# Attention layer of a two-layer streaming step: which queue loads what was turned through DRAM, when the values are loaded, and when the second group's outputs are turned

## The chip, the cores and the metric

The kernel runs on one core of one Trainium2 chip. The metric is the device time of one execution in microseconds (us); the time before is the median of three runs. Five engines work side by side, each through its own instructions in order: TensorE (PE in the profile; PEld is its weight load), VectorE (DVE), ScalarE (ACT), GpSimd (POOL) and SyncE (SP). SP computes nothing here: it issues the transfers (DMAs). ACT can issue transfers too, from the same stream of instructions in which its computing stands. A transfer that has to wait for data waits in the stream of the engine that issues it.

## The reference

One inference step of a trunk with two layers, for a prompt of 512 tokens and a sample of 32 (T = 544 columns). Layer 0 mixes tokens by a recurrence (RWKV-7); layer 1, which the change touches, by differential attention. Cut to layer 1:

```python
h = rmsnorm(x, norm_w)
q, k, v, qm, gate = jnp.split(h @ w_in, [MIX_W, 2 * MIX_W, 3 * MIX_W, 3 * MIX_W + MEM_W], axis=-1)
...
attn = probs(q1, k1) - lam * probs(q2, k2)
return jnp.einsum('bhqk,bkhd->bqhd', attn.astype(v_all.dtype), v_all)
...
o = rmsnorm(o, subln) * (1.0 - lam_init)
y_mem = mem_attention(qm, mk, mv)
out = jnp.concatenate([o.reshape(B, T, MIX_W).astype(x.dtype), y_mem], axis=-1) * jax.nn.silu(gate)
return x + out @ w_out, k, v
```

There are 12 heads of 128, in three groups of four; scores are masked to chunks of 64. Four memory heads attend to 256 memory rows.

## The kernel before

**Products.** A projection is three float32r products (high by high, high by low, low by high part) over 8 blocks of 128 rows, for two halves of 272 columns: 48 products for each block of 128 output columns. Each head of layer 1 has blocks for its values, keys and queries, most have a gate block, and heads 1, 3, 5 and 7 have two more for a memory head. So a head takes 144, 192, 240 or 288 products; even heads 0 to 8 take 192.

**The written order.** `diff_layer` (L1809) puts all other work between these products by hand. `at(pos, fn)` (L1817) has `fn` called ahead of product `pos`; `f` is the first product of a head. One loop calls what is due and then issues the next product. With `self.ordered` set, `tie` (L142) keeps each engine's instructions in the order in which they are called: `self.te`, `self.ve`, `self.ae` and `self.se` are the queues of PE, DVE, ACT and SP. All instructions called through these have line L125 in the profile, so that one reads by the names of tiles instead.

**One head.** Scores of four tiles of 128 queries are computed at `f + x`, their exponentials on ACT at `f + x + 6`, and at `f + y` (`TILES1`, L39) DVE joins the two maps and turns the result, the weights, in 32 by 32 blocks into `pk`. The rest of the turn goes through DRAM. With `y` = 280 for the last tile:

- `weights_out` (L1955), 24 products after `y`: four stores `ptr<-pk`;
- `weights_back` (L1964), `BACK1` = 88 after `y`: the values (`values_back`, L1960: `vt<-scr`), then the turned weights (`aT<-ptr`), both issued by SP;
- `weighted` (L1969), `SUMS1` = 160 after `y`: 20 products `ps_o<-vt,aT`, which DVE copies to `ot`.

`vt`, `aT` and the staging tile `to` have one buffer each. Heads 10 and 11 have `BACK2` and `SUMS2`; head 10 stores at 8 after `y`, and head 11 turns its weights on PE and loads its values alone.

Since a head of 192 products ends before `y` + 24, the later steps of a head lie among those of the next: for the even heads the weights are stored at product 112 of the next head, just behind that head's `keys_out` at 108 (`kh<-kh`, two copies, and four stores `scr<-sg`).

**Other turns through DRAM.** DVE turns a tile in blocks into `to`, SP stores it (`spread`, L1784), and SP loads it back: the cached keys (`cached_back`, L2015), the memory heads' weights (`mem_steps`, L1131; four loads `mpT<-mspread` for each of four memory heads, 56 products after the last stores and 62 ahead of their use) and the first group's outputs (`turned_back`, L2088: `oTt<-spread`, 60 products after the stores, 42 ahead of their use in `finished`).

**Outputs.** When a group's four heads are done, `norms` computes their scales at product `b`; `scaled` (L2078) multiplies each head's output `ot` by them, and `finished` (L2092) multiplies it into the gates `og`. The first group is turned through DRAM, the second and third by PE (`ps_oT<-ident,ot`, four transposes per head in one PSUM bank of a pair shared with the memory heads' products, `ps_mo`, and `ps_o`). For the second group `b` is product 76 of head 9; head j is scaled at `b` + 18 + 14j and turned at `b` + 30 + 24j. A memory head's `ps_mo` is written at product 120 of head 9.

Of the kernel before, what the change touches and what calls it, by code (L numbers as in the profile page):

```python
# [17 lines left out]
P = 128  # L18
D = 1024
KT = D // P  # L20
TP = 512
TS = 32
# [12 lines left out]
DH = 12  # L35
# [6 lines left out]
SAMPLE1 = ((310, "s"), (338, "m"), (362, "t"), (386, "w"), (406, "n"), (464, "r"))  # L42
SAMPLE2 = ((186, "s"), (214, "m"), (228, "t"), (264, "w"), (311, "n"), (336, "r"))
TILES2 = ((152, 180), (210, 236), (240, 268), (272, 304))
BACK1, SUMS1, NORM1 = 88, 160, 52
BACK2, SUMS2, NORM2 = 56, 104, 34
SUMS3 = 22
NORM1B = 76
OTURN = 1
# [4 lines left out]
OUT1 = 24  # L54
# [73 lines left out]
class Trunk:  # L128
# [1002 lines left out]
    def mem_steps(self, st, i, h, p):  # L1131
# [64 lines left out]
        else:  # L1196
            pT = p.tile([P, 2, T], F32, tag="mpT", name="mpT")
# [9 lines left out]
        if i and MTURN:  # L1207
            yield
            pT = p.tile([P, 2, T], F32, tag="mpT", name="mpT")
            for j in range(2):  # L1210
                x = scr.rearrange("(t j p) q -> j p t q", j=2, p=P)[j]
                self.se.dma_start(pT[:, j, :TP].rearrange("p (t q) -> p t q", t=4), x[:, :4])
                self.se.dma_start(pT[:, j, TP:], x[:, 4, P - TS :])
        yield
        sg = st["gate"]()
        g = self.dest(12 + h, sg)
# [592 lines left out]
    def diff_layer(self, dq, p, mp, mctx, pool_early, order, made):  # L1809
# [7 lines left out]
        def at(pos, fn):  # L1817
            ev.append((pos, len(ev), fn))
# [13 lines left out]
        def make_v(st):  # L1832
            def make(w):
                st["v"] = dq.tile([P, T], F32, tag="v", name="v", bufs=KB)
                yield from self.steps(w, copied(st["v"]))
            return make

        def make_k(st):
            def make(w):
                st["k"] = dq.tile([P, T], F32, tag="k", name="k", bufs=KB)  # L1840
                yield from self.steps(w, copied(st["k"]))
            return make
# [16 lines left out]
        def make_gate(g):  # L1859
            def make(w):  # L1860
                yield from self.steps(w, self.gate_evac(self.o1[g])[2])
            return make
# [97 lines left out]
        def values_back(st):  # L1960
            st["vt"] = vt = p.tile([P, 4, P], F32, tag="oTt" if st["h"] == DH - 1 else "vt", name="vt", bufs=1)
            self.se.dma_start(vt[:], st["G"]["scr"][1][:TP, st["j"], :].rearrange("(i p) d -> p i d", p=P))

        def weights_back(st):  # L1964
            st["aT"] = aT = p.tile([P, 10, P], F32, tag="aT", name="aT", bufs=1)
            values_back(st)
            self.se.dma_start(aT[:], st["ptr"].rearrange("(i b) t c -> (b t) i c", b=4))

        def weighted(st):  # L1969
            G, j = st["G"], st["j"]  # L1970
# [17 lines left out]
        def opened(G, hg):  # L1988
            G["scr"] = [self.dp.tile([T, 4, P], F32, tag=f"scr{i}", name=f"scr{i}", bufs=3) for i in range(2)]
            G["on"] = []  # L1990
# [23 lines left out]

        def cached_back(G):  # L2015
            ckT = p.tile([P, 4, P], F32, tag="ckT", name="ckT")
            self.se.dma_start(ckT[:], G["ckT"].rearrange("(j d) q -> d j q", d=P))
            G["ckT"] = ckT

        def sample_scores(G):  # L2020
# [66 lines left out]

        def turned_back(G, j):  # L2088
            G["oT", j] = x = p.tile([P, 4, P], F32, tag="oTt", name="oTt", bufs=1)
            self.se.dma_start(x[:], G["ot", j].rearrange("(t d) q -> d t q", d=P))  # L2090

        def finished(G, hg, j):  # L2092
            if hg < OTURN:
                x = G.pop(("oT", j))[:].rearrange("p t q -> p (t q)")
            else:
                ps = self.psm.tile([P, 512], F32, tag="m", name="ps_oT")
                for t in range(4):
                    self.te.transpose(ps[:, t * P : t * P + P], G["on"][j][:, t, :], self.ident[:])
                x = ps[:]
            g = self.o1[4 * hg + j]  # L2100
            self.ve.scalar_tensor_tensor(g[:, :TP], x, self.subs, g[:, :TP], ALU.mult, ALU.mult)
            self.ve.tensor_tensor(g[:, TP:], G["oT"][:, 32 * j : 32 * j + 32], g[:, TP:], ALU.mult)
# [10 lines left out]
        for h, st in enumerate(sts):  # L2113
            f, hg, G = len(makes) * 6 * KT, h // 4, groups[h // 4]
            start.append(f)
            makes += [make_v(st), make_k(st), make_q(st)] + [make_gate(g) for g in GATES1.get(h, ())]
            if h % 4 == 0:
                at(f, lambda G=G, hg=hg: opened(G, hg))
                at(f + 97, lambda G=G: sample_open(G))
                at(f + 152, lambda G=G, hg=hg: cached(G, hg))  # L2120
            if h % 4 == 1:
                for off, fn in ((4, cached_keys), (14, cached_stored), (78, cached_back)) if CTURN else ((124, cached_turned),):
                    at(f + off, lambda G=G, fn=fn: fn(G))
            for off, fn in ((52, values_turn), (62, lambda st: st["vout"]()), (99, keys), (108, keys_out)):
                at(f + off, lambda st=st, fn=fn: fn(st))
            last = h == DH - 1
            for t, (x, y) in enumerate(TILES2 if last else TILES1):
                at(f + x, lambda st=st, t=t: scores(st, t))
                at(f + x + 6, lambda st=st, t=t: powers(st, t))
                at(f + y, lambda st=st, t=t, fn=joined if last else turned: fn(st, t))  # L2130
                if last:
                    at(f + y + 12, lambda st=st, t=t: turned_here(st, t))
            back, sums = (BACK2, SUMS2) if h >= DH - 2 else (BACK1, SUMS1)
            for off, fn in ((124, values_back),) if last else ((y + (8 if h == DH - 2 else OUT1), weights_out), (y + back, weights_back)):
                at(f + off, lambda st=st, fn=fn: fn(st))
            at(f + y + (SUMS3 if last else sums), lambda st=st: weighted(st))
            at(f + y + (SUMS3 + 11 if last else sums + 14), lambda st=st: squared(st))
            if h in MEM1:
                m = MEM1.index(h)
                makes += [make_query(mems[m]), make_mem_gate(mems[m], m)]  # L2140
                for off in MEMAT1:
                    at(f + off, lambda m=m: next(mits[m], None))
            if h % 4 == 3:
                for off, fn in (SAMPLE2 if last else SAMPLE1):
                    fn = {"s": sample_scores, "m": sample_mixed, "t": sample_turned, "w": sample_weighted, "n": sample_norm, "r": sample_rows}[fn]
                    at(f + off, lambda G=G, fn=fn: fn(G))
                b = f + y + NORM2 if last else begin(h + 2) + (NORM1 if h < 4 else NORM1B)
                at(b, lambda G=G: norms(G))
                for j in range(4):
                    if hg >= OTURN and not last:  # L2150
                        at(b + 18 + 14 * j, lambda G=G, j=j: scaled(G, j))
                        at(b + 30 + 24 * j, lambda G=G, hg=hg, j=j: finished(G, hg, j))
                    elif last:
                        at(b + 18 + 8 * j, lambda G=G, j=j: scaled(G, j))
                        at(b + 30 + 14 * j, lambda G=G, hg=hg, j=j: finished(G, hg, j))
                    else:
                        x = b + 18 + STEP * j
                        at(x, lambda G=G, j=j: (scaled(G, j), turned_out(G, j)))
                        at(x + 10, lambda G=G, j=j: turned_stored(G, j))
                        at(x + GAP1, lambda G=G, j=j: turned_back(G, j))  # L2160
                        at(x + GAP2, lambda G=G, hg=hg, j=j: finished(G, hg, j))
            if h == 10:
                we = []
                at(f + 34, lambda: (mctx.close(), we.append(pool_early())))
            if h >= 10:
                def early(g):
                    made[g] = self.gated(g, *self.fetch(we[0], g))

                def late(g, n):
                    if n == 3:  # L2170
                        hi, lo = (dq.tile([P, T], F32R, tag=x, name=x + "hl", bufs=KB)[:] for x in "kv")
                    else:
                        t = self.kz[0] if n == 2 else dq.tile([P, 2, T], F32R, tag=("qp", "kh")[n], name="hl", bufs=QB)
                        hi, lo = t[:, 0, :], t[:, 1, :]
                    made[g] = self.gated(g, hi, lo, self.o1[g][:])
                for i in range(2):
                    at(f + 40 + 60 * i, lambda g=order[2 * h - 20 + i]: early(g))
            if last:
                for i in range(4):
                    at(f + LATE[i], lambda g=order[4 + i], i=i: late(g, i))  # L2180
# [102 lines left out]
```

## Time and profile before

| | |
|---|---|
| median of 3 runs | 1376.84 us (1376.33 to 1378.81) |
| the profiled execution's own time | 1376.32 us |
| its span, from the first instruction to the last | 1374.6 us |
| layer 1's attention, by PE's products | about 827 to 1268 us of the span |

The profile is one execution. A row of the timeline has start, duration, engine, line, operation, output<-inputs, shape, count, and in brackets the idle time of the engine before it and what ended it. A row of the chain of waits has start, duration and what the time went to. A row of the windows has the stretch, its length, then for each engine the busy time and the number of instructions, then PE's granted clock, the busy share of the 16 DMA engines and GB/s; it can be made for one tile's instructions alone. A row of waits has who waited for whom, the sum, the count and the longest, in us. Since matmuls are pipelined, products that follow each other closely overlap in the rows: one takes some 290 ns from start to end, but the next starts 125 ns after it.

In the issues of the page, one `aT<-ptr` moves 640 KB, one `vt<-scr` 256 KB, one `ptr<-pk` 160 KB, and the four `mpT<-mspread` of a memory head 256, 16, 256 and 16 KB.

### The profile page before, as it was taken

Reading aid. Unit: us, or ns where it says so; the run is one execution under the profiler, and the core shown is the slowest. Engines: PE = TensorE matmul, PEld = TensorE weight load, DVE = VectorE, ACT = ScalarE, POOL = GpSimd, SP = SyncE. Lnnn points to the kernel's source line nnn. Section 1 sums busy time; section 2 is a strip of 40 time slices with the busy share of each in tenths; the row PEclk is TensorE's granted clock in tenths of the full one; section 3 lists DMA queues with packets and bytes.
Section 4 is the critical chain, followed back from the end, with each engine's and each line's share of the span. In section 5 each row is a group of like instructions: output and inputs, shape, how many; then the busy total and the mean of one; then the engine's idle time right before and its main releaser. Section 6 shows DMA issues by size and latency. Waiting matters only on the chain. (4 is left out here: it accounts for less than half of the span.)

```text
span 1374.6 us, 31283 instructions
## 1 busy us (share of the span) xinstructions
PE 1323.3 (96%) x11584; PEld 1267.4 (92%) x11584; DVE 896.9 (65%) x2207; ACT 773.1 (56%) x2090; POOL 567.3 (41%) x986
## 2 busy tenths in 40 slices
PE   6999999999999999999999999999999999999997
PEld 6998899999999999888899999999999899899997
DVE  7776667877787778756674473555667456767443
ACT  7665677677777776655643354544444354454321
POOL 2317675558556855560130034444343343442000
PEclk9999999999999999999999999999999999999998
DMA  7542223322332232323273457676888688785321
GB/s 237 176 128 68 65 64 83 85 74 64 84 86 73 63 85 76 77 81 110 87 219 122 132 154 185 164 173 163 205 181 182 169 202 184 161 187 171 93 70 65
DMA packets 428850, 173.57 MB, mean 126 GB/s; under 512 B 203721, under 2 KB 413138, under 8 KB 428698
## 3 DMA queue, kind: packets, MB, share of 16 engines
q1 hardware_dynamic: 428554, 171.06, 48.1%
q8 instruction: 91, 1.49, 0.4%
q10 hardware_dynamic: 144, 0.52, 0.1%
q14 instruction: 61, 0.50, 0.1%
HBM read 131.89 MB, written 42.96 MB: 127 GB/s over the span
## 5 line engine op out<-in xcount | busy, mean ns | idle before, releaser
L125 PE MATMUL ps_g<-hl,whi 128*128 128x272 f32 x1872 | 544.4, 294 | 0.6 <-POOL hl L497 0.5
L125 PE MATMUL ps_g<-hh,wlo 128*128 128x272 f32 x1808 | 537.0, 297 | 1.4 <-DVE wlo L125 1.4
L125 PE MATMUL ps_g<-hh,whi 128*128 128x272 f32 x1808 | 536.5, 297 | 0.9 <-ACT hh L125 0.9
L125 PEld LDWEIGHTS ps_g<-hl,whi 128*128 128x128 f32 x1872 | 352.8, 190 | 3.2 <-POOL hl L497 0.7
L125 PEld LDWEIGHTS ps_g<-hh,whi 128*128 128x128 f32 x1808 | 343.3, 190 | 5.3 <-ACT hh L125 1.3
L125 PEld LDWEIGHTS ps_g<-hh,wlo 128*128 128x128 f32 x1808 | 342.8, 190 | 5.7 <-DVE wlo L125 2.2
L125 ACT CAST whi<-raw 128x512 fp32r<-128x512 f32 x322 | 190.9, 619 | 92.4 <-PE ps_g L125 51.3
L786 POOL TENSOR_TENSOR tm<-u,m 102x84 f32<-102x84 f32 (+23 forms) x372 | 154.6, 416 | 167.3 <-DMA m<-sc 139.2
L335 POOL TENSOR_TENSOR wlo<-raw,whi 128x512 fp32r<-128x512 f32 x110 | 142.9, 1316 | 191.4 <-ACT whi L125 168.0
L125 DVE TENSOR_TENSOR wlo<-raw,whi 128x512 fp32r<-128x512 f32 x212 | 153.8, 741 | 65.4 <-ACT whi L125 63.9
L788 POOL TENSOR_TENSOR u<-u,tm 102x84 f32<-102x84 f32 (+23 forms) x372 | 165.5, 445 | 29.1
L125 PE MATMUL ps_g<-lo,whi 128*128 128x272 f32 x448 | 129.3, 289 | 0.7 <-DVE lo L125 0.7
L125 PE MATMUL ps_g<-hi,whi 128*128 128x272 f32 x448 | 129.2, 288 | 0.0
L125 PE MATMUL ps_g<-hi,wlo 128*128 128x272 f32 x448 | 129.1, 288 | 0.0
L125 PEld LDWEIGHTS ps_g<-lo,whi 128*128 128x128 f32 x448 | 84.2, 188 | 1.1 <-DVE lo L125 1.1
L125 PEld LDWEIGHTS ps_g<-hi,whi 128*128 128x128 f32 x448 | 84.3, 188 | 0.0
L125 PEld LDWEIGHTS ps_g<-hi,wlo 128*128 128x128 f32 x448 | 84.3, 188 | 0.0
L125 DVE SCALAR_TENSOR_TENSOR SB<-ps_c,dl,sd 64x64 f32<-64x64 f32 x168 | 47.5, 282 | 45.1 <-PE ps_c L125 40.1
L125 ACT COPY sv<-ps_c 64x64 f32<-64x64 f32 x192 | 39.5, 206 | 37.6 <-PE ps_c L125 35.8
L1882 POOL TENSOR_TENSOR kz<-k,kh 64x544 fp32r<-64x544 f32 x24 | 33.0, 1373 | 51.4 <-ACT kh L125 50.5
L1652 POOL TENSOR_TENSOR hl<-hn,hh 128x544 fp32r<-128x544 f32 x8 | 12.5, 1568 | 92.9 <-ACT hh L125 92.9
L125 DVE SCALAR_TENSOR_TENSOR qp<-ps_g,qp 64x272 fp32r<-64x272 f32 x48 | 21.1, 439 | 41.4 <-ACT qp L125 41.2
(397 smaller groups left out, 2566.0 us busy)
## 6 DMA issues: line engine op xcount, KB each, us to landing
raw<-in_rw_in_dram SPq DMA_DIRECT2D x114, 256.0 KB
raw<-in_df_in_dram SPq DMA_DIRECT2D x112, 256.0 KB
raw<-in_w_out_dram SPq DMA_DIRECT2D x64, 256.0 KB
ptr<-pk SPq DMA_DIRECT2D x44, 160.0 KB
aT<-ptr SPq DMA_DIRECT2D x11, 640.0 KB
scr<-sg SPq DMA_DIRECT2D x96, 68.0 KB
out_dram<-scr SPq DMA_DIRECT2D x6, 1024.0 KB
m<-sc SPq DMA_DIRECT2D x36, 128.0 KB
```

What stands on the lines that cost most here:

```text
L125: return lambda *a, **k: self.trunk.tie(self, issue(*a, **k))
L335: todo.append((lambda k=k, q=q: low.tensor_tensor(lo[:, k], raw[q][:], hi[:, k].bitcast(F32), ALU.subtract), LATER))
L786: nc.gpsimd.tensor_tensor(tm[:, :n, :wd], u3[:, :n, kx : kx + 1].to_broadcast(sh), m3[:, kx : kx + 1, kx + 1 :].to_broadcast(sh), ALU.mult)
L788: nc.gpsimd.tensor_tensor(u3[:, :n, kx + 1 :], u3[:, :n, kx + 1 :], tm[:, :n, :wd], ALU.add)
L1652: nc.gpsimd.tensor_tensor(self.hl[:, k, :], h[:], self.hh[:, k, :].bitcast(F32), ALU.subtract)
L1882: nc.gpsimd.tensor_tensor(self.kz[h % 2][rows[m], m, :], k[rows[m], :], hi.bitcast(F32), ALU.subtract)
```

## The change

Four edits, all in layer 1:

- the loads of `aT`, `mpT`, `ckT` and `oTt` are issued by ACT (`self.ae`) in place of SP (`self.se`), at the same places of the order; `aT`'s load is 4 products earlier (`BACK1` 88 to 84; `BACK2` 56 to 54);
- the values of heads 0 to 10 are loaded 18 products after `y`, in place of `BACK1` or `BACK2`: ahead of the weights' stores, except in head 10, which stores at 8; still by SP;
- head 10's (and only its) `SUMS2` is 112 in place of 104;
- the second group's outputs are turned at `b` + 54 + 24j in place of `b` + 30 + 24j.

```diff
-BACK1, SUMS1, NORM1 = 88, 160, 52
-BACK2, SUMS2, NORM2 = 56, 104, 34
+BACK1, SUMS1, NORM1 = 84, 160, 52
+BACK2, SUMS2, NORM2 = 54, 112, 34
...
-                self.se.dma_start(pT[:, j, :TP].rearrange("p (t q) -> p t q", t=4), x[:, :4])
-                self.se.dma_start(pT[:, j, TP:], x[:, 4, P - TS :])
+                self.ae.dma_start(pT[:, j, :TP].rearrange("p (t q) -> p t q", t=4), x[:, :4])
+                self.ae.dma_start(pT[:, j, TP:], x[:, 4, P - TS :])
...
         def weights_back(st):
             st["aT"] = aT = p.tile([P, 10, P], F32, tag="aT", name="aT", bufs=1)
-            values_back(st)
-            self.se.dma_start(aT[:], st["ptr"].rearrange("(i b) t c -> (b t) i c", b=4))
+            self.ae.dma_start(aT[:], st["ptr"].rearrange("(i b) t c -> (b t) i c", b=4))
...
-            self.se.dma_start(ckT[:], G["ckT"].rearrange("(j d) q -> d j q", d=P))
+            self.ae.dma_start(ckT[:], G["ckT"].rearrange("(j d) q -> d j q", d=P))
...
-            self.se.dma_start(x[:], G["ot", j].rearrange("(t d) q -> d t q", d=P))
+            self.ae.dma_start(x[:], G["ot", j].rearrange("(t d) q -> d t q", d=P))
...
-            for off, fn in ((124, values_back),) if last else ((y + (8 if h == DH - 2 else OUT1), weights_out), (y + back, weights_back)):
+            for off, fn in ((124, values_back),) if last else ((y + min(18, back - 2), values_back), (y + (8 if h == DH - 2 else OUT1), weights_out), (y + back, weights_back)):
...
-                        at(b + 30 + 24 * j, lambda G=G, hg=hg, j=j: finished(G, hg, j))
+                        at(b + 54 + 24 * j, lambda G=G, hg=hg, j=j: finished(G, hg, j))
```

## The prediction

> **What bounds the kernel now.** First the page, then the waits of TensorE (PE) in the attention layer, 826 to 1270 us.
>
> ```profile
> span 1374.6 us, 31283 instructions
> PE 1323.3 (96%) x11584; PEld 1267.4 (92%) x11584; DVE 896.9 (65%) x2207; ACT 773.1 (56%) x2090; POOL 567.3 (41%) x986
> PE ps_o L125 <- DMA aT<-ptr: 4.7, 3, 3.0
> PE ps_oT L125 <- DVE ot L125: 2.3, 2, 1.9
> PE ps_s L125 <- DMA kh<-kh: 0.8, 1, 0.8
> PE ps_oT L125 <- DVE og L125: 0.6, 1, 0.6
> PE ps_s L125 <- ACT pt L125: 0.4, 1, 0.4
> ```
>
> PE is busy for 96%, and its products are issued in one written order. So a saving must come out of the 51 us in which PE is idle, and only 8.8 us of those (the sum of the five wait rows) lie in the layer that the change touches. The timeline of PE places them; the windows view shows what follows the longest.
>
> ```profile
> 920.04 0.30 PE L125 MATMUL ps_s<-kh,qp 128*128 128x128 f32 x1 [0.85 <-DMA kh<-kh]
> 1034.67 0.44 PE L125 MATMUL ps_s<-kh,qp 128*128 128x384 f32 x1 [0.41 <-ACT pt L125]
> 1039.71 2.47 PE L125 MATMUL ps_o<-vt,aT 128*128 128x128 f32 x20 [0.54 <-DMA aT<-ptr]
> 1072.35 3.32 PE L125 MATMUL ps_o<-vt,aT 128*128 128x128 f32 x20 [2.97 <-DMA aT<-ptr]
> 1118.94 2.39 PE L125 MATMUL ps_o<-vt,aT 128*128 128x128 f32 x20
> 1152.49 2.47 PE L125 MATMUL ps_o<-vt,aT 128*128 128x128 f32 x20 [1.22 <-DMA aT<-ptr]
> 1170.88 0.66 PE L125 MATMUL ps_oT<-ident,ot 128*128 128x128 f32 x4 [1.87 <-DVE ot L125]
> 1177.33 0.66 PE L125 MATMUL ps_oT<-ident,ot 128*128 128x128 f32 x4 [0.62 <-DVE og L125]
> ...
> 1020.00:1040.00 20.00, 19.05 (x149) 18.64 (x148) 11.49 (x32) 9.38 (x29) 9.53 (x8) 1.00 0.99 220
> 1060.00:1080.00 20.00, 17.03 (x126) 16.84 (x126) 8.37 (x20) 8.13 (x21) 9.56 (x7) 0.91 0.78 175
> ...
> 1075.67 0.91 PE ps_g L125 x4
> 1042.18 0.76 PE ps_g L125 x6
> ```
>
> In the window that holds the 2.97 us gap the granted clock is 0.91; in the window with the 0.54 us gap it is 1.00. The twenty products behind the long gap take 3.32 us where the undisturbed twenty take 2.39, and four weight products take 0.91 where six took 0.76 (four: 0.51). So this wait costs 2.97 + 0.93 + 0.40, about 4.3 us, not 3.0.
>
> **Why the weights come late.** The timeline of SyncE (SP), heads 4, 5 and 7, and the products that PE ran ahead of head 5's wait:
>
> ```profile
> 1023.42 3.57 SPq L125 DMA_DIRECT2D ptr<-pk  x4
> 1028.08 1.26 SPq L125 DMA_DIRECT2D oTt<-spread  x1
> 1033.58 0.50 SPq L125 DMA_DIRECT2D aT<-ptr  x1
> 1051.37 3.21 SPq L125 DMA_DIRECT2D ptr<-pk  x4
> 1060.79 2.63 SPq L125 DMA_DIRECT2D scr<-sg  x4
> 1063.52 1.87 SPq L125 DMA_DIRECT2D raw<-in_df_in_dram  x1
> 1065.49 0.45 SPq L125 DMA_DIRECT2D vt<-scr  x1
> 1066.00 0.50 SPq L125 DMA_DIRECT2D aT<-ptr  x1
> 1131.95 4.05 SPq L125 DMA_DIRECT2D ptr<-pk  x4
> 1145.54 0.58 SPq L125 DMA_DIRECT2D aT<-ptr  x1
> ...
> 1060.17:1069.40 9.23, 9.21 (x74) 8.99 (x72) 1.31 (x3) 2.03 (x6) 1.00 0.75 172
> ...
> 1066.00 6.22 DMA aT<-ptr
> 1150.69 3.10 DMA mspread<-to
> ```
>
> The load is written 72 products ahead of its use (88 against 160). PE passed that place at 1060.2: the window holds 74 products, two of them at its edges. SP issued it at 1066.00, since it stood behind a store that waited, four stores and a weight load that waited. It landed 6.22 us later, at 1072.2; PE had stood since 1069.4. SP was 5.8 us late, and that, not the transfer alone, is the wait.
>
> **The change, part by part.** (1) *aT to ScalarE's (ACT's) queue*, 11 issues. It now starts when ACT gets to the place and the weights' stores have landed. Store landing isn't a row; the nearest is the 3.10 us of a store out of the same kind of transpose, the far end the 6.22 of aT. Head 5: stores issued by 1054.6, landed about 1057.7. ACT's position:
>
> ```profile
> 1060.20 0.39 ACT L125 COPY k<-ps_g 128x272 f32<-128x272 f32 x1
> 1027.42 0.40 ACT L125 ACTIVATE og<-ps_g 128x272 f32<-128x272 f32 x1
> 1032.59 0.75 DVE L125 SCALAR_TENSOR_TENSOR og<-oTt,dv,og 128x512 f32<-128x512 f32 x1 [3.18 <-DMA oTt<-spread]
> ```
>
> ACT reaches it at 1060.6, the data lands at 1066.8 with the old 6.22, and PE comes at 1069.4: 2.6 us to spare. Head 7: stores issued by 1136.0, landed 1139.1; PE passes the place about 9 us + scores ahead of 1151.3, so the load goes near 1140.5 rather than 1145.54; 6 us later is 4.5 us early. Head 4: stores landed about 1030.1, load then rather than at 1033.58, landing 1036.3 against 1039.2. All three waits go: 0.54 + 2.97 + 1.22 = 4.7 us, and 1.3 us at the low clock with them. Together **6.0** (ends: 2.8, if only the longest shrinks, by half, and the low clock goes with it, and 6.0 itself).
>
> The clock drop is the place to weigh the Trainium skill: its page "TensorE: Matmul & The Clock Gate", section "What's actually happening", has the half rate follow one idle window of about 3.4 us. The 2.97 us gap here is shorter, so by the page the 1.3 us need not go with the wait, and the sum below would be 6.2 in place of 7.5; the trace has the drop behind this gap and none behind those of 1.87 us and less, and I go by the trace.
>
> (2) *Values ahead of the weights' stores* (SP, 11 issues of 0.45 to 0.50 us, some 70 products earlier). Their single buffer is free: the last user's products are written 50 products before, two before in head 10, and SP comes to them no sooner than PE, if it runs as late as at head 5. They put 0.5 us of issue and 256 KB ahead of the stores, so weights land up to 1.5 us later; counted in (5). In odd heads they also stand just ahead of the keys' copies. Head 10's products, 8 later with their load, had no wait: nothing.
>
> (3) *Other loads to ACT*: the first group's outputs (4), cached keys (3), memory weights (16). With aT, SP loses 34 issues of about 0.5 us, 17 us; POOL issues no load in this layer and is passed by none. The outputs' load is the one that now hurts: VectorE stood 3.18 us for it, came late to the scores' maxima, and so PE waited 0.41. It is written 42 products (5.3 us) ahead of its use, which VectorE came to at 1029.4; so ACT issues it near 1024.1 rather than SP at 1028.08, and with the old 4.5 us to its use it is there at 1028.6: **0.4** saved (0 to 0.4). Where SP runs ahead of PE, the memory weights now go later, when ACT gets there; the 62 products (7.8 us) to their use cover the 6.22 us that a load of two and a half times their size takes: nothing, at worst 1 us for each of four heads. The keys' copy behind the wait of 0.85 had the values and weights of the head before just ahead of it on SP; the weights now share the engines instead of standing in front, and I take half: **0.4** (0 to 0.85; in odd heads up to -1).
>
> (4) *Second group's outputs turned 24 products on* (3.0 us, 16 transposes, 8 VectorE instructions, moved past a pair of score tiles; VectorE is busy for 65% of the span).
>
> ```profile
> 1157.44 0.71 DVE L125 STREAM_TRANSPOSE to<-ck 128x512 f32<-128x512 f32 x1 [3.08 <-DMA mspread<-to]
> 1170.09 0.73 DVE L125 TENSOR_TENSOR ot<-ot,oss 128x512 f32<-128x512 f32 x1
> ```
>
> VectorE lost 3.08 us to a store and scaled the first output at 1170.09; PE had come at 1169.0. 3.0 us later the tile is ready with 1.2 us to spare, so 1.87 goes. The 0.62 is a wait for a PSUM bank that the memory head's output still holds, 10 products before; with the new places the first output follows that output by the same 10 products, so half of it may stay. **2.2** (0 to 2.5).
>
> (5) *What ACT pays.* A wait now stands in ACT's stream: behind it are PSUM copies, exponentials and weight casts, for which PE, VectorE and POOL wait. Head 4: ACT is free at 1027.8, the stores land at 1030.1 to 1030.6; held 2.5 us. The far end, 6.22 for the stores, holds it 5.4. The even heads have their stores at the same place, right behind the keys' copies, and are taken alike; head 5 isn't held (1057.7 against 1060.6). PE needs an exponential 32 products (4 us) after its scores, and has three banks of 24 products: 2.5 us mostly fits. I take **-1.5** in all (0 to -6: four heads by 1.5). The issues themselves:
>
> ```profile
> 1260.46 2.01 ACTq L1708 DMA_DIRECT2D fw<-in_final_norm_w_dram  x1
> 1260.66 0.38 ACT L125 ACTIVATE og<-ps_g 128x272 f32<-128x272 f32 x1
> L125 SPq DMA_DIRECT2D aT<-ptr x11: 359/497/579, 878.3 to 1233.5; - x11
> ```
>
> The one issue on ACT took 2.01 us, the same transfers on SP 0.5. ACT went on computing beside its issue, and is idle 44% of the time; I take 0.5 us each, hidden.
>
> **Sum.** 6.0 + 0.4 + 0.4 + 2.2 - 1.5 = 7.5 us off the profiled execution's 1376.32 (1.7 us more than its span): 1368.8. The median shown is 0.5 above that execution: **1369.3**. Ends of this case: 1366.5 to 1372.
>
> **Rivals.**
> *ACT is held longer than PE's banks cover.* The stores land by the 6.22 us row; each of four even heads costs PE 1 to 1.5 us, some 5 us instead of 1.5: 1373. For: the stores are many short runs, and the values now go ahead of them. Against: the 4 us between scores.
> *The loads land no earlier.* In 1020 to 1040 the DMA share is 0.99, so a load issued earlier only queues in the engines. Then (1) shrinks to the issue time of what no longer precedes it, about 1.5 us, (3) gives nothing and (4) 2.2, less 1.5 for ACT: 1374.6. Against: the share around the longest wait is 0.75 to 0.78. The Trainium skill stands with this rival: "DMA: Bandwidth & Descriptors", section "Issuing engines are not separate DMA queues", says that issuing from several engines saves only the sequencer's issue time, usually small. Here that time was 5.8 us for head 5.
> *Slower: ACT's issues cost 2.01 us each.* Four in a row for a memory head hold ACT 8 us, against 6 us of banks: 2 us lost, four times; aT's adds 1.5 us to each of four held heads, beyond the 4 us between scores: 14 us lost against 9.0 gained, and 1381.8. It decides from about 1.2 us an issue. Against: ACT computed beside its 2.01 us.
>
> **Chances.** Forecast 0.62; held longer 0.17; no earlier 0.12; slower 0.09. I count as no change what lies within 0.2% (2.75 us) of 1376.84, about what a measurement of this kernel can tell. The forecast is faster; of the second case 0.13 is faster, 0.04 the same; of the third 0.03 and 0.08, with 0.01 slower. Faster 0.78, same 0.12, slower 0.10. The range of 8 in 10 leaves out the slower case and the upper part of the third: 1365.5 to 1374.5, the low end 1 us below the case's, for the spread of single runs.
>
> **What would show it.** aT on ACT's queue, issued near 1030, 1060 and 1140; no ps_o row with a wait, clock 1.00 throughout; the ps_oT wait of 1.87 gone. Wrong, if PE waits for ACT's exponentials or bank copies behind a load, if aT takes much longer than 6.2 us to land, or if ACT's issue rows are near 2 us.

## The result, and the profile after

The change made the kernel slower: 1391.49 us (median of 4 runs, 1390.65 to 1392.18) against 1377.25 for the kernel before in the same session, a ratio of 1.0104 (1.0090 to 1.0118). The forecast was 1369.3. The profiled execution's span went from 1374.6 to 1389.7 us, 15.1 more. From the first to the last of layer 1's 2688 written products PE took 448.6 us instead of 433.3; what follows them took the same (114.3 and 114.6). That first number, the *layer time*, is read from PE's rows in every run below.

The row of the page on the engines:

```profile
PE 1326.9 (95%) x11584; PEld 1270.1 (91%) x11584; DVE 894.5 (64%) x2207; ACT 771.8 (56%) x2090; POOL 564.7 (41%) x986
```

PE is busy 3.6 us longer for the same products, which is the low clock, and idle for 62.8 us instead of 51.3. Its waits in the attention layer (826 to 1290 us: who waited for whom, sum, count, longest):

```profile
PE ps_o L125 <- DMA aT<-ptr: 7.5, 3, 5.2
PE ps_s L125 <- DMA kh<-kh: 5.9, 5, 2.4
PE ps_o L125 <- issue: 1.7, 1, 1.7
PE ps_g L125 <- DVE srs L125: 1.5, 1, 1.5
PE ps_s L125 <- ACT pt L125: 0.6, 1, 0.6
PE ps_oT L125 <- DVE og L125: 0.5, 1, 0.5
PE ps_oT L125 <- DVE ot L125: 0.2, 1, 0.2
```

The three old waits for `aT` are gone (heads 4, 5 and 7: 0.54, 2.97 and 1.22 us before), and that of 1.87 for `ot`. But the largest row is again `aT`, now in heads 0, 2 and 6 (0.3, 5.2 and 2.0 us), where nothing waited before, and the keys' copies, waited for once and 0.8 us before, are waited for five times. The seven rows make 17.9 us where the five of before made 8.8.

The chain of waits shows the two longest transfers of the turned weights, in heads 2 and 6, and one of keys, in head 8:

```profile
955.56 13.36 DMA aT<-ptr
1120.26 11.42 DMA aT<-ptr
1153.88 5.96 DMA kh<-kh
```

Head 2's load, which in the kernel before took 5.9 us on SP's queue (issued at 953.6, landed at 959.5), took 13.36 us on ACT's. What moved in that stretch, 955.2 to 969 us, stands in the view of the DMA queues (packets, MB, share of the 16 engines; then the issues). q1 carries what SP issues, q10 what ACT issues:

```profile
q1 hardware_dynamic: 3963, 3.62, 78.8%
q10 hardware_dynamic: 1296, 0.66, 16.1%
out_dram<-scr SPq DMA_DIRECT2D x2, 1024.0 KB
raw<-in_df_in_dram SPq DMA_DIRECT2D x3, 256.0 KB
aT<-ptr ACTq DMA_DIRECT2D x1, 640.0 KB
```

So the load met the copies of keys and values to the outputs (`out_dram<-scr`). On a queue of its own it ran *beside* them, and while SP's queue moved 3.62 MB, it got 16% of the engines for its 0.66. In the kernel before, the copies came on SP's queue 10.4 us behind the load, when it had landed. SP's three rows there:

```profile
953.56 0.37 SPq L125 DMA_DIRECT2D aT<-ptr  x1
953.98 9.96 SPq L125 DMA_DIRECT2D raw<-in_df_in_dram  x4
963.99 3.14 SPq L125 DMA_DIRECT2D out_dram<-scr  x4
```

and the copies' row in the changed kernel:

```profile
955.29 3.40 SPq L125 DMA_DIRECT2D out_dram<-scr  x4
```

Between load and copies stood four loads of the projections' weights (`raw`), three of which waited for POOL. The load's leaving is not all that changed here. Counted by the `raw` loads issued ahead of them, the copies of heads 2 and 6 also moved up by three places in SP's own stream. The kernel calls them behind the layer (`kv_out`, when `self.ordered` is off), so that no `tie` holds them at a place. No run has the load on ACT with the copies at their old place.

The second new thing is in SP's waits and ACT's in the layer (826 to 1290 us):

```profile
SPq L125 <- DMA aT<-ptr: 30.7, 7, 7.1
SPq L125 <- DMA oTt<-spread: 3.5, 2, 2.3
SPq L125 <- DMA mpT<-mspread: 3.0, 3, 1.6
SPq L125 <- DMA ckT<-spread: 2.5, 1, 2.5
ACT cmk L125 <- DMA ptr<-pk: 11.6, 3, 5.8
```

SP issues none of these four loads and uses none of their data, yet it stands 39.7 us until they have landed. The events of the trace show why. Each transfer of the two queues counts its end on one of eight semaphores, which the program hands round over both queues: in the kernel before, the 430 transfers issued from 826 to 1260 us use the eight in turn without a break, and in the changed kernel ACT's loads use the same eight. When SP comes to a semaphore whose last transfer was ACT's, its instruction waits until that transfer has landed: each of SP's waits above is for the very semaphore on which its next transfer counts. In the kernel before, where one queue issued everything, SP waited less than 2 us for transfers in this layer.

At last the clock. Windows of PE around head 2's gap and head 6's (columns as before: busy time and count of PE, granted clock, DMA share, GB/s):

```profile
963.00:967.00 4.00, 0.87 (x7) 1.00 1.09 374
967.00:969.00 2.00, 0.00 (x0) 0.51 0.41 123
971.00:974.00 3.00, 3.00 (x16) 0.52 0.08 23
...
1085.00:1087.00 2.00, 1.42 (x9) 0.88 0.86 128
1087.00:1089.00 2.00, 2.00 (x10) 0.50 0.76 195
```

The clock was half from 967.0 to 973.9 us, around the end of the gap of 5.2, and for 3.4 us each behind gaps of 1.33 (head 6's keys) and 2.36 (head 8's).

### The profile page after: what moved, and what is told of

The parts are those of the page before. It is cut to its first block, busy times and chain, and to the rows that moved or that the text cites. A ratio compares the mean times of both kernels' runs of the same rounds, so it can differ in the third digit from the quotient of the medians.

```text
span 1389.7 us, 31324 instructions
## 1 busy us (share of the span) xinstructions
PE 1326.9 (95%) x11584; PEld 1270.1 (91%) x11584; DVE 894.5 (64%) x2207; ACT 771.8 (56%) x2090; POOL 564.7 (41%) x986
## 5 line engine op out<-in xcount | busy, mean ns | idle before, releaser
L788 POOL TENSOR_TENSOR u<-u,tm 102x84 f32<-102x84 f32 (+23 forms) x372 | 160.8, 432 | 29.1
```

The source lines that it names most:

```text
L788: nc.gpsimd.tensor_tensor(u3[:, :n, kx + 1 :], u3[:, :n, kx + 1 :], tm[:, :n, :wd], ALU.add)
```

## The experiments

The theories: **Q**, the load on a second queue shares the engines with what SP's queue has under way, and lands late; **S**, SP waits on the shared semaphores until ACT's loads have landed, and then issues keys and stores late; **H**, ACT, which waits for the stores ahead of its load, comes late with exponentials and copies; **V**, the values in front delay stores and keys.

Each ratio is to the kernel before on the same chip, with its 95% interval. "SP for ACT" is the time that SP waited in the layer for loads issued by ACT. A layer time is that of the one profiled execution, and so less sure than a median: the one of at_act took 1387.19 us and that of sp_copies_last 1367.19, each some 3 us under its median.

| run | median us | ratio | layer time us | SP for ACT us |
|---|---|---|---|---|
| the change | 1391.49 | 1.0104 (1.0090 to 1.0118) | 448.6 | 39.7 |
| sp_all | 1372.50 | 0.9961 (0.9944 to 0.9978) | 429.6 | 0 |
| sp_all_again | 1371.94 | 0.9957 (0.9945 to 0.9970) | 429.8 | 0 |
| at_act | 1390.22 | 1.0099 (1.0069 to 1.0128) | 445.0 | 24.3 |
| others_act | 1378.80 | 1.0010 (0.9995 to 1.0025) | 436.4 | 7.3 |
| turn54 | 1374.69 | 0.9984 (0.9969 to 0.9999) | 430.8 | 0 |
| vals_early | 1374.38 | 0.9986 (0.9977 to 0.9996) | 430.1 | 0 |
| tiny_act | 1377.56 | 1.0005 (0.9994 to 1.0016) | 433.4 | 15.4 |
| tiny_dep | 1370.59 | 0.9958 (0.9943 to 0.9972) | 430.0 | 2.6 |
| after_at_pool | 1412.10 | 1.0256 (1.0241 to 1.0271) | 471.8 | 8.3 |
| copies_last | 1380.64 | 1.0019 (1.0008 to 1.0031) | 436.5 | 24.8 |
| sp_copies_last | 1370.46 | 0.9948 (0.9933 to 0.9963) | 427.0 | 0 |
| best_gap58 | 1370.58 | 0.9953 (0.9939 to 0.9966) | 429.2 | 0 |

### The queue, or the rest of the change: sp_all, at_act, others_act

sp_all is the changed kernel with all four loads back on SP:

```diff
-            self.ae.dma_start(aT[:], st["ptr"].rearrange("(i b) t c -> (b t) i c", b=4))
+            self.se.dma_start(aT[:], st["ptr"].rearrange("(i b) t c -> (b t) i c", b=4))
```

and the same for `mpT`, `ckT` and `oTt`. at_act is the kernel before with this line alone the other way (the values stay right ahead of it, on SP); others_act is the kernel before with the other three loads on ACT.

> The changed kernel with all 34 loads put back on SP's queue; the values ahead of the weights' stores, the 84/54 products and the second group's later turn stay. Theory (the loads on ACT's queue cost the time: SP stands 30.7 us for weights and 9.0 us for the other loads that ACT issued, and the weights land in 7.7 to 13.4 us beside SP's copies): SP's waits for loads are gone, no head's weights take over 7 us, PE's waits for kh are back at about 1 us, the ps_oT wait of 1.87 is gone, and the time is 1372 to 1377, at or below before. Rival (the values ahead of the stores delay the stores and the keys' copies): the PE waits for kh of 5.9 us stay for the most part, and the time is 1383 to 1388.

> The kernel before with one edit: the load of the turned weights (11 issues) is issued by ACT. Theory S (SP waits until a load that ACT issued has landed, where its own next DMA counts on the same semaphore): SP's waits for aT are again some 25 to 35 us, PE waits for kh and for aT, and the time is 1381 to 1387. Theory Q (no more than the loss of the place ahead of SP's copies): aT lands in 8 to 13 us in three or four heads, PE waits for aT 5 to 8 us and for kh as before (1 us), 1379 to 1383. Theory H (ACT held until the stores have landed): PE waits for ACT and VectorE, 2 to 3 us; alone it gives 1375 to 1378, as the waits of 4.7 us for aT go.

> The kernel before with one edit: the first group's turned outputs, the cached keys and the memory weights (23 issues) are issued by ACT, the weights by SP as before. Theory S: SP waits some 9 us for these loads, in short pieces of 1 to 2.5 us, keys come late in one or two heads: 1377 to 1380. Rival (these loads are harmless, and only aT costs): PE's waits as before, 1376 to 1378; the waits of 0.41 for pt gone at best.

PE's waits in sp_all:

```profile
PE ps_s L125 <- ACT pt L125: 2.0, 2, 1.8
PE ps_s L125 <- DMA kh<-kh: 1.0, 2, 0.5
```

These are the two largest rows. None is left for `aT`, the keys are at 1.0 us, and the kernel is 0.4% *faster* than before. The second profile of this kernel, sp_all_again, does have a row for `aT`:

```profile
PE ps_o L125 <- DMA aT<-ptr: 2.1, 2, 1.3
```

So a difference of 2 us in such a row between two profiles can be one of executions and not of kernels. By the times V falls, and the whole loss, some 19 us between the change and sp_all, comes with the loads' move to ACT. at_act puts most of it on `aT`: with 11 loads moved it is 13 us slower than before. Its SP waits:

```profile
SPq L125 <- DMA aT<-ptr: 24.3, 8, 5.0
```

and head 2's load in the chain of waits:

```profile
953.32 10.65 DMA aT<-ptr
```

That bears out S and Q both; the time of 1390 lies above what either gave. In this kernel the values, behind SP's waits, come late too (PE waited 3.8 us for `vt`). In others_act the interval holds no change. Its profile shows how such a wait travels: SP waited 2.15 us for `oTt` just ahead of head 4's stores of weights, and PE then 3.27 us for that head's `aT`.

### The two parts that stayed on SP: turn54, vals_early

```diff
-                        at(b + 30 + 24 * j, lambda G=G, hg=hg, j=j: finished(G, hg, j))
+                        at(b + 54 + 24 * j, lambda G=G, hg=hg, j=j: finished(G, hg, j))
```

is turn54; vals_early takes `values_back(st)` out of `weights_back` and adds `(y + min(18, back - 2), values_back)` to the list ahead of `weights_out`.

> The kernel before with one edit: the second group's outputs are turned 24 products later. If the prediction's step on it holds: the ps_oT wait of 1.87 goes, that of 0.62 at least by half, nothing else moves: 2 us, 1375.0 to 1375.8. Rival (the group only moves against other work, VectorE or the banks are late elsewhere): same waits at another place, 1377.

> The kernel before with one edit: the values are loaded ahead of the weights' stores (SP, 88/56 products as before). Between it and the later turn lies the whole of sp_all's gain of 4.6 us; turn54 alone gave 2.4. If the two parts simply add: 1374.5 to 1376, the waits for aT of 0.5, 3.0 and 1.2 shorter by about 0.5 us each (the issue that no longer precedes aT). Rival (the values in front delay the stores' landing by as much): waits for aT as before, 1377.

turn54 gives 2.4 us, vals_early 2.6, and sp_all, which holds both, 4.6 and 5.6 in its two sessions: within the noise they add. In turn54 the wait for `ot` fell from 2.3 us to 0.5, that for `og` stayed at 0.6. In vals_early the waits for `aT` are down from 4.7 us in three to 1.8 in two:

```profile
PE ps_o L125 <- DMA aT<-ptr: 1.8, 2, 1.6
```

### S and H without Q: tiny_act, tiny_dep

Both are sp_all, in which `aT` comes by SP, plus one row of 512 bytes that ACT loads at each of the 11 places and nobody reads:

```diff
+            x = p.tile([1, P], F32, tag="tiny", name="tiny", bufs=1)
+            self.ae.dma_start(x[:], a["norm_w"][0:1, 0:P])
```

tiny_dep reads `st["ptr"][0, 0:1, :]` instead, so that ACT has to wait for the stores.

> sp_all, with a load of one row of 512 bytes on ACT's queue added at the place of each of the 11 weights' loads; it reads an input, waits for nothing and nobody reads it, so aT's landing is untouched (Q excluded) and ACT is not held (H excluded). Theory S (SP must wait until ACT's load has landed, where its own DMA comes to the same semaphore, even before ACT has come to the place): SP has waits for this load, 1 to 3 us each in some heads, 5 to 15 us in sum, and the time is 1373 to 1376. Rival (SP waited only because aT took long): no wait of over 0.5 us, 1372 to 1373.

> As tiny_act, but the small load reads a row of the stored weights, so that ACT waits for the stores to land as it does in the changed kernel, while aT itself is loaded by SP. Theory S: SP's waits grow by what ACT is held, to 10 to 20 us in sum; theory H: ACT waits for the stores 8 to 15 us and PE or VectorE for ACT, 1 to 3 us over tiny_act; together 1375 to 1379. If Q alone makes the loss (aT long in the engines beside SP's copies): as sp_all, 1372 to 1374.

In tiny_act SP waits for these loads, and PE for the keys behind them. SP's waits:

```profile
SPq L125 <- DMA tiny<-in_norm_w_dram: 15.4, 9, 2.6
```

Head 7's place in the timelines of SP, ACT and PE:

```profile
1140.82 3.91 SPq L125 DMA_DIRECT2D mspread<-to  x4
1142.63 0.22 ACTq L125 DMA_DIRECT2D tiny<-in_norm_w_dram  x1
1149.20 0.30 PE L125 MATMUL ps_s<-kh,qp 128*128 128x128 f32 x1 [1.87 <-DMA kh<-kh]
```

The four stores take 3.91 us, since one of them (at 1144.43) waited 2.02 us for a semaphore that the load of 512 bytes held; the keys' copy behind them was issued at 1145.36 and PE stood. The longest wait of PE in this trace is another, in head 5:

```profile
1074.91 3.88 PE L125 MATMUL ps_o<-vt,aT 128*128 128x128 f32 x20 [2.54 <-issue]
```

SP issued that head's `aT` behind a wait of 1.01 us for a load of 512 bytes. How much of the 2.54 us comes from it is not shown: sp_all_again, without such loads, waited 1.33 us at this place.

Eleven transfers that carry next to nothing cost 5 us against sp_all by the medians (1377.56 to 1372.50) and 3.8 by the layer time. So S is real and has a price of its own, even where ACT's transfer is short: SP had run ahead of ACT in the written order, and was pulled back to it.

tiny_dep was a surprise for S and a clear answer for H. Its waits (SP, then ACT):

```profile
SPq L125 <- DMA tiny<-ptr: 2.6, 2, 1.7
ACT cmk L125 <- DMA ptr<-pk: 10.8, 3, 4.7
```

ACT is held by the stores as long as in the changed kernel (10.8 and 11.6 us at the same copy), and the time is no longer than that of sp_all: **holding ACT costs nothing by itself** that the times show. SP waits only twice. The trace shows the difference: in tiny_act the semaphore's next user was the very next transfer to be issued in eight of eleven cases, since SP had run ahead and stood; in tiny_dep four to six others were issued between in eight of eleven. Why the load has a later place in the hand-round there was not tested.

### Another queue with semaphores of its own: after_at_pool

The changed kernel with `aT` issued by POOL (`self.nc.gpsimd.dma_start`).

> The changed kernel with aT's loads on POOL's queue in place of ACT's. If S holds and that queue's DMAs count on other semaphores, SP's waits for aT (30.7 us) are gone, PE's waits for kh shrink from 5.9 to 1 to 2 us; by theory Q aT still lands in 8 to 13 us beside SP's copies and PE's waits for aT stay at 5 to 8 us: 1380 to 1386. If SP's wait is of another kind than the shared semaphores, SP still waits 25 to 35 us for aT, and the time is 1388 or more. POOL is held by the stores in ACT's place; its weight remainders (wlo), for which SP's weight loads wait, may come 2 to 5 us later.

The waits of PE and SP:

```profile
PE ps_o L125 <- DMA aT<-ptr: 16.3, 5, 5.6
PE ps_o L125 <- issue: 15.6, 4, 5.9
SPq L125 <- POOL wlo L335: 113.1, 48, 8.9
SPq L125 <- DMA oTt<-spread: 3.7, 2, 2.7
```

SP's waits for `aT` are gone, and PE's for the keys with them; those for `oTt` and the others, still on ACT, stay. That is S's signature. But it is 21 us slower than the change, beyond what I had written: POOL came to its place late, behind remainders that wait for ACT (head 1's load was issued at 915.90 instead of 908.16), and the remainders came late in turn, for which SP's weight loads wait (113.1 us, 65.3 in sp_all).

What I had expected of Q did not come. In heads 2 and 6 the loads met the same copies, and landed in 7.5 and 7.7 us. The DMA queues from 965.1 to 972.7 us, head 2:

```profile
q1 hardware_dynamic: 1335, 1.43, 56.2%
q0 software_dynamic: 176, 0.66, 26.2%
out_dram<-scr SPq DMA_DIRECT2D x2, 1024.0 KB
aT<-ptr POOLq DMA_DIRECT2D x1, 640.0 KB, 7.5
```

POOL's queue moved the same 0.66 MB in 176 packets (3.7 KB each) where ACT's took 1296 (0.5 KB each), and while it did so, in 7.6 us, SP's queue moved 1.43 MB, where it moved 3.62 in the 13.8 us of the change. So two queues and a large copy are not enough for 10 us and more: in the change it was a load in small packets beside SP's larger ones (3963 for 3.62 MB, 0.9 KB each).

That the packets decide it is a reading of these rows; no run changed their size alone. A rival is that SP issued its two large copies further apart here: the second came 6.3 us (head 2) and 4.2 us (head 6) behind the load, against 1.0 and 1.9 in the change. Head 10 of the change speaks against it: there the second came 5.0 us behind the load, and on ACT's queue the load still took 10.1 us.

### Q: copies_last, sp_copies_last

The twelve output copies are tied behind the layer's last transfer on SP, in the changed kernel and in sp_all:

```diff
-            self.se.dma_start(o[4 + i][0, 0, :, 4 * hg : 4 * hg + 4, :], scr[:TP])
-            self.se.dma_start(o[10 + i][0, 0, :, 4 * hg : 4 * hg + 4, :], scr[TP:])
+            for x, y in ((o[4 + i], scr[:TP]), (o[10 + i], scr[TP:])):
+                self.order(self.se.dma_start(x[0, 0, :, 4 * hg : 4 * hg + 4, :], y), done[0])
...
+        done = [self.se.last]
         self.ordered = False
```

> The changed kernel, with the twelve copies of keys and values to the outputs (up to 1024 KB each, read and write together; in heads 2, 6 and 10) tied behind the layer's last DMA on SP, so that they no longer run beside aT's load on ACT's queue. Theory Q (aT takes 13.4, 11.4 and 10.1 us in those heads because these copies on SP's queue share the engines with it): aT lands in 5 to 8 us there, the wait of 5.2 us for it in head 2 falls to 1 us or less with its clock drop, SP's waits for aT fall from 30.7 to some 20 to 25 us, PE's waits for kh stay at 4 to 6 us, and the time is 1383 to 1387, less what the copies cost at their new place. Rival (other transfers do it, or ACT's late issue): aT still takes 9 us and more, 1390 to 1393.

> sp_all with the same twelve copies tied behind the layer: what the copies' new place costs or gives by itself, where aT goes ahead of them on SP's queue anyway. Expected: nothing in heads 2 and 10 (PE waited for nothing there), up to 3 us lost behind the layer if the copies delay the output's loads: 1371 to 1375.

In copies_last `aT` lands 6.3, 6.8 and 6.7 us after its issue in heads 2, 6 and 10, instead of 13.4, 11.4 and 10.1. The DMA queues from 954.2 to 960.8 us, head 2's load:

```profile
q1 hardware_dynamic: 1973, 0.98, 51.2%
q10 hardware_dynamic: 1296, 0.66, 34.6%
```

The waits of SP and PE:

```profile
SPq L125 <- DMA aT<-ptr: 15.0, 4, 4.8
PE ps_s L125 <- DMA kh<-kh: 6.8, 5, 2.7
PE ps_g L125 <- DVE srs L125: 1.5, 1, 1.5
```

and head 8's keys in the chain of waits:

```profile
1143.69 5.69 DMA kh<-kh
```

No row for `ps_o` is left. The layer time falls by 12.1 us against the change, 2.6 of which the copies' move gives by itself (sp_copies_last against sp_all; 1.5 by the medians, against sp_all_again, with intervals that overlap). So some 9.4 are Q by the copies. What is left between copies_last and sp_copies_last, 9.5 us in the layer and 10.2 in the medians, is the price of ACT's queue without them. Of that, 4.5 lies in head 8: PE's wait of 2.7 for the keys and the half clock behind it. There the keys' copy took 5.69 us beside head 7's `aT` (5.96 in the change, 6.08 in at_act, but 3.7 in tiny_act and 3.6 in sp_copies_last, where `aT` came behind it on SP). So most of this wait is again sharing. The rest, 5 us, is spread over heads 1 to 6 in pieces of 0.8 to 1.8 (less 0.7 in head 9): keys that SP issued late, and 1.5 us for DVE.

### A better version: best_gap58

```diff
-STEP, GAP1, GAP2 = 60, 70, 112
+STEP, GAP1, GAP2 = 60, 58, 112
```

in sp_all.

> sp_all with the first group's turned outputs loaded 12 products earlier (58 in place of 70 behind their scaling, still behind the use that frees their buffer), so that on SP they go ahead of a weight load that waited 1.92 us. In sp_all VectorE stood 4.88 us for the first of them and PE 1.75 us for pt behind it, with a stretch at the low clock. If that wait was SP's order: 1 to 2 us faster than sp_all, 1370 to 1372. Rival (the load waits for the buffer or the stores' landing instead): as sp_all.

> sp_all once more, beside best_gap58 on the same chip: 1371 to 1374, 0.994 to 0.998 of the kernel before.

In best_gap58 PE's wait for `pt` was 1.1 us, against 2.0 in sp_all and 2.5 in sp_all_again. For `aT` it waited 2.6 us, against none and 2.1. The intervals of best_gap58, sp_all_again and sp_copies_last overlap. Three versions are 0.4 to 0.5% faster than the kernel before and 1.4 to 1.5% faster than the change; which of them is best the runs do not tell.

## Why the prediction was wrong

1. *"the data lands at 1066.8 with the old 6.22"*, and so 6.0 us gained: **this is the step that failed first.** It was right where no output copies ran: head 5's load landed in 6.0 us, and the old waits of heads 5 and 7 are gone. But the 6.22 us were a duration with none of the output copies under way, and nothing in the sum asked where these copies, which no `tie` holds, would come. Beside them it was 13.4, 11.4 and 10.1 us, and heads 2, 6 and 10 got waits that they had not had, 5.2, 2.0 and 1.7 us (the last as "issue"), with up to 6.8 us at half clock. copies_last shows that cause by taking the copies away. I looked at the DMA share around the waits that the change was to remove, and not around the other eight loads.
2. *"With aT, SP loses 34 issues of about 0.5 us, 17 us"*: **the second failed step, and a wrong sign.** SP's stream got 39.7 us of waits in exchange. I listed what a wait adds on ACT, and named nothing that would wait for ACT's loads but their readers. The semaphores' hand-round was in the trace of before, as ids; no wait came of it there, since one queue issued everything. tiny_act prices it at 5 us for loads of 512 bytes.
3. *The keys' copy, "the weights now share the engines instead of standing in front, and I take half": 0.4 gained.* PE's wait for keys went from 0.8 to 5.9 us. In head 8 the weights on SP came *behind* the keys' copy; moved to ACT they came beside it.
4. *Values ahead of the stores*, counted at no gain and as a delay of the weights by up to 1.5 us: too low. Alone they gave 2.6 us (vals_early), and in that run's profile the waits for `aT` are shorter.
5. *The later turn, 2.2 us*: right, 2.4 (turn54; its interval reaches from 0.1 to 4.3). The wait of 1.87 went as written; that of 0.62, of which half was to go, stayed.
6. *ACT held, -1.5; issues 0.5 us each, hidden*: the issues were 0.37 us (median of 11), so the slower rival with 2.01 us an issue was wrong in its price, though its side was the one that came. ACT was held longer than the 2.5 us written for head 4 (5.8 there), but holding costs nothing by itself (tiny_dep). The 1.5 us of DVE in head 4 comes from late stores (`spread<-to`): SP had stood 2.26 us for `oTt` ahead of them, and DVE stood 6.97 us until they had landed.

The rival "the loads land no earlier" had the right mechanism, sharing, and the wrong floor: it took for granted that a load on another queue lands no *later*. The Trainium skill stood with it ("DMA: Bandwidth & Descriptors", section "Issuing engines are not separate DMA queues": transfers of all engines interleave on the same 16 engines, and another issuer saves only issue time). The trace agrees, with 16% of the engines for `aT` beside 79%. The 5.8 us that I set against this rival were SP's lateness at head 5, not the time to issue one load, which was 0.5 us. No range that I gave reached 1391: for that, one of the two failed steps had to be a rival of its own.

Put together, from the layer times: later turn and values, 3.7 us gained (433.3 to 429.6); sharing with the output copies, 9.4 lost; head 8's keys, mostly sharing, 4.5; SP's and ACT's waits elsewhere, 5.0. That makes the 15.2 that were lost (433.3 to 448.6). It must, since all four are differences of the same layer times: this is a split of the loss, not a second proof of it. How the last 5.0 divide between SP's waits and other sharing stays open; tiny_act's 5 us are at other places.

## What to carry to other kernels

Moving a load to a second queue frees it from what stands ahead of it, but it also gives up its place ahead of what stands behind: look up, for each of its executions, what the old queue has under way in the time of the transfer, not only where the load was late. Look also at the order that the new program has: transfers that nothing ties to a place can move, as the output copies did. Before you split transfers over two issuing engines, look at which semaphores they count on: if both engines share them, the one that runs ahead is held until the other's transfers have landed. Split a change into its parts: here two of them were worth 5 us, and the third cost 19.

## What the runs showed of the hardware

In the changed kernel a load of 640 KB took 10.1 to 13.4 us beside two copies of 1024 KB on the other queue, and 4.5 to 7.7 us in the eight heads without them; the two queues did not share the engines by halves (16.1% and 78.8% in head 2). On POOL's queue, in packets seven times as large, the same load took 7.5 and 7.7 where it met these copies.

PE's clock fell to half for 3.4 us behind gaps of 1.33 and 2.36 us in the changed kernel and of 1.75 us in sp_all, but not behind one of 1.97 us in turn54, so the length of one gap did not decide. sp_all's window behind the gap that ended at 1036.2:

```profile
1038.00:1040.00 2.00, 2.00 (x10) 0.50 1.14 318
```

and turn54's behind the one that ended at 1070.1:

```profile
1070.00:1072.00 2.00, 1.92 (x17) 1.00 0.73 198
```

Ten products in one, seventeen in the other, and turn54's clock stayed full in this layer. The Trainium skill's page "TensorE: Matmul & The Clock Gate", section "What's actually happening", has the half rate follow about 3.4 us without work; these drops came after less, and the measurement decides. All changes of the clock in one trace lie whole multiples of 3.41 us apart: the three drops of the changed kernel came at 967.03, 1086.50 and 1161.59 us, the last two 35 and 57 such steps behind the first. So it matters also where among these steps a gap falls. In the step that ended with each drop PE was idle for 3.2, 1.4 and 1.8 us in all; but steps with 1.5 and 1.7 us of idle time passed without a drop, so this sum alone does not decide either. A gap of 1.3 us can thus cost 3 us, and one of 2.0 only itself.
